# Ordering the modulation matmuls of a two-layer diffusion backbone on TensorE

## The chip, the cores and the metric

One core of one Trainium2 chip runs the whole program in one launch. The metric is device microseconds from the first to the last instruction of that core. The time before is the median of three runs, 2419.5 us (2418.51 to 2420.97).

## What is computed

Two streams of 128 tokens (context and latent) go through two trunk layers with the same weights. Each layer normalises its input, shifts and scales it by a vector that comes from a conditioning vector, makes one wide projection, runs three mixers on its columns, projects and merges their outputs, and adds the result to its input under a gate:

```python
mod = c_silu @ w_mod[l] + b_mod[l]                      # [1, 3*2048] of each stream
shift, scale, gate = jnp.split(mod, 3, axis=-1)
h = rms_norm(x, p['norm_w'][l]) * (1 + scale[:, None, :]) + shift[:, None, :]
(... 12 groups of columns ...) = split_columns(h @ p['w_in'][l])
# HGRN2 recurrence, grouped-query attention, S5 state-space scan
merged = (g_hg * (o_hg @ p['w_br_hg'][l]) + g_at * (o_at @ p['w_br_at'][l]) + g_s5 * (o_s5 @ p['w_br_s5'][l]))
x = x + gate[:, None, :] * (merged @ p['w_out'][l])
```

`mod` is what the change is about: one row of each stream times a matrix of 2048 x 6144, for each of the two layers. All values are float32.

## The kernel before

**The large products** are in `gemm` (lines 160 to 181). A piece of weights, `raw`, is 128 x 1024 (two chunks of 128 rows by 512 columns, 512 KB). SyncE issues its load; three `raw` buffers exist. Each chunk is split into a high part `wh` (a cast on ScalarE, line 138) and a low part `wl` (a subtraction on VectorE, line 139), four buffers each. TensorE then makes six matmuls of 128 x 512 for a chunk (lines 178, 179, 180 for each of the two streams), into a PSUM tile `g`. There are 672 pieces and 8064 of these matmuls.

**The modulation** is in `mod_part` (lines 244 to 295). `w_mod` is cut in six parts a layer, of 1024 columns each, and sixteen chunks of 128 rows. Since only two rows are on the left, a chunk is done as four matmuls, each with 32 columns of the array and 256 columns of the weights, at `tile_position=(0, 32 * i)`: four of them stand side by side in the array and write four partition blocks of one PSUM tile `mod`. A run of chunk pairs is summed in PSUM, and VectorE adds the sum to `bm` (line 276). The first part of layer 0 is done before everything else, parts 1 to 3 run beside the first columns of the projection, one pair of chunks (8 matmuls) at a time. The other eight parts (the gate of layer 0 and all of layer 1) run as *side work* of the later `gemm` calls: a generator is advanced by a rate, and each step loads four chunks (`MB = 2` pairs) and makes their 16 matmuls: 32 bursts of 16. Their weights `wm` go into buffers of 128 x 1024 that the tags `k4` (three buffers) and `q4` (two) hold, which other tiles use as well: five chunks at most stand ready at a time. The loads are issued by SyncE, in one queue with those of `raw`.

**The order** on each engine is made by a scheduler that simulates the program: of the instructions that are ready in its simulated time it takes the one with the lowest priority number. `self.prio(base)` numbers what stands in it from `base` upwards in order of writing. Loads and splits have `P_TOP` (1,000,000), the matmuls of `gemm` and those of the side work `P_PE` (6,000,000), the S5 scan on VectorE `P_SCAN` (500,000), and `P_MIX` is 0. An engine works its instructions in that order and waits where one is not ready.

**The S5 scan** (line 820 on) is 64 dependent steps of four VectorE instructions (lines 825, 827, 830, 831), made eight times in all; `bu` matmuls (line 813) feed it, and `yp` matmuls (lines 837 and 844) on TensorE need its end.

Of the kernel before, what the change touches and what calls it, by code (L numbers as in the profile page):

```python
# [52 lines left out]
P_MIX = 0  # L53
# [8 lines left out]
class Builder:  # L62
# [65 lines left out]

# [1 line left out]
    def transpose4(self, src, n=4, ps=None):  # L130
# [29 lines left out]
    def gemm(self, pieces, hi, lo, nk):  # L160
        """hi(k), lo(k): [128, 256] stationary parts of both streams; pieces: DRAM APs [128, 1024]."""
        nc = self.nc
        ps = [self.pg.tile([128, 512], F32, tag="g", name=self.nm("g")) for _ in range(2)]
        for kk, src in enumerate(pieces):
            self.side_work()
            with self.prio(P_TOP):
                raw = self.wp.tile([128, 2, 512], F32, tag="raw", name=self.nm("raw"), bufs=RAW)
                nc.sync.dma_start(raw, src.rearrange("p (a b) -> p a b", a=2))
            for j in range(2):
                with self.prio(P_TOP):  # L170
                    wh = self.wp.tile([128, 512], F32R, tag="wh", name=self.nm("wh"))
                    wl = self.wp.tile([128, 512], F32R, tag="wl", name=self.nm("wl"))
                    self.split_from(raw[:, j], wh, wl)
                k = 2 * kk + j
                with self.prio(P_PE):
                    for s in range(2):
                        sl = slice(s * 128, s * 128 + 128)
                        nc.tensor.matmul(ps[s], lo(k)[:, sl], wh, start=(k == 0), stop=False)  # L178
                        nc.tensor.matmul(ps[s], hi(k)[:, sl], wh, start=False, stop=False)  # L179
                        nc.tensor.matmul(ps[s], hi(k)[:, sl], wl, start=False, stop=(k == nk - 1))  # L180
        return ps

    def rstd(self, ssq, n, width):
        """1/sqrt(ssq/width + eps), with one Newton step after the table's square root."""
        nc = self.nc
        v = self.ts("v", (128, n))
        y = self.ts("y", (128, n))
        r = self.ts("r", (128, n))
        w = self.ts("w", (128, n))
        nc.vector.tensor_scalar(v, ssq, 1.0 / width, EPS, ALU.mult, ALU.add)  # L190
        nc.scalar.activation(y, v, AF.Sqrt)
        nc.vector.reciprocal(r, y)
        nc.vector.tensor_mul(w, r, r)
        nc.vector.tensor_mul(w, w, v)
        nc.vector.tensor_scalar(w, w, -0.5, 1.5, ALU.mult, ALU.add)
        nc.vector.tensor_mul(r, r, w)
        return r

# [1 line left out]
    def condition(self):  # L200
# [41 lines left out]

# [1 line left out]
    def mod_part(self, l, part, prio, tags, plan):  # L244
        """A sixth of c @ w_mod for both streams, two k chunks at a time; four column blocks side by side.

        Parts 0 to 3 are shift and scale of a quarter of the channels, 4 and 5 the halves of the gate. plan: runs
        of chunk pairs that are summed in PSUM, (bank, pairs, pairs between two yields)."""
        nc, io = self.nc, self.io
# [5 lines left out]
        for bank, run, burst in plan:  # L255
            ps = None
            for k0 in range(kb, kb + run, burst):
                ws = []
                for k in range(k0, k0 + burst):
                    with self.prio(P_TOP):  # L260
                        tag, n = next(tags)
                        for i in range(0, 2, n):
                            w = self.t(tag if isinstance(tag, str) else tag[i], "wm", (128, n * 1024))
                            nc.sync.dma_start(w, io["w_mod"][l, part, k][:, i * 1024:(i + n) * 1024])
                            ws += [w[:, j * 1024:(j + 1) * 1024] for j in range(n)]
                with self.prio(prio):
                    if ps is None:
                        pool = dict(g=self.pg, m=self.pm, b=self.pb)[bank]
                        ps = pool.tile([128, 512], F32, tag=bank, name=self.nm("mod"))
                    for k in range(2 * k0, 2 * (k0 + burst)):  # L270
                        for i in range(4):
                            nc.tensor.matmul(ps[32 * i:32 * i + 32, 0:256], self.cT[:, 2 * k:2 * k + 32],  # L272
                                             ws[k - 2 * k0][:, i * 256:i * 256 + 256], start=(k == 2 * kb),
                                             stop=(k == 2 * (kb + run) - 1), tile_position=(0, 32 * i))
                    if k0 + burst == kb + run:
                        nc.vector.tensor_add(bm, bm, ps[:, 0:256])
                if k0 + burst < 8:
                    yield True
            kb += run
# [16 lines left out]

# [1 line left out]
    def square(self, ssq, x, s, n):  # L298
# [9 lines left out]
    def normed(self, x, rs, q):  # L308
        """Channels 512 q .. 512 q + 511 of both streams."""
        nc = self.nc  # L310
# [20 lines left out]
    def in_group(self, l, name, idx, k0=0, k1=16):  # L331
        """Channel chunks k0 .. k1 - 1 of one group of columns."""
        pieces = [self.io["w_in"][l, GIDX[name, idx], kk] for kk in range(k0 // 2, k1 // 2)]
# [7 lines left out]
    def begin(self, l, name, idx, q):  # L341
        """A quarter of the channels' share of a group, put where the whole will stand."""
        ps = self.in_group(l, name, idx, 4 * q, 4 * q + 4)
# [40 lines left out]

# [1 line left out]
    def hgrn_unit(self, l, s, hf, q, f, v, og):  # L386
        """Four heads of one stream. q, f[2] (sigmoids), v: [128 tokens, 512]; og: output slice [128, 512].

        Pairs (s, t) are covered by a binary tree over time: at level m the queries of one half of every
        2m-block meet the keys of the other half; QF/KB carry the decay from the block's inner edge."""  # L390
        nc, io = self.nc, self.io
# [97 lines left out]

# [1 line left out]
    def head_norm(self, x, nh, w):  # L491
# [22 lines left out]
    def attention(self, l, s, q, kv, og):  # L514
        """q: [128, 8, 128], kv: [128, 512] (2 key heads, 2 value heads); og: [128, 1024]."""
        nc, io = self.nc, self.io
# [57 lines left out]

# [1 line left out]
    def vexp(self, x, n, wk):  # L576
        """exp on the vector engine to float32 accuracy."""
        nc = self.nc
# [60 lines left out]
    def s5_params(self, l):  # L639
        """Discretised per-state coefficients of both directions.  # L640

        The scan runs over pairs of tokens: state' = a^2 state + (a B u_first + B u_second)."""
        nc, io = self.nc, self.io
# [61 lines left out]
    def s5_input(self, l, qd, Bl, C, Sb):  # L705
        """Input matrices of one quarter, block-diagonal over two groups, the odd token's part stacked on the
        even one's; built in the scan's buffer before the scan needs it."""
        nc, io = self.nc, self.io
# [34 lines left out]
    def s5_output(self, l, qd, C, CC, cb):  # L743
        """C a of both directions, and C B + diag(d), which joins a token to its own output."""
        nc = self.nc
# [18 lines left out]
    def s5_half(self, l, hh, us, ys):  # L764
        """Channels of chunks 4*hh .. 4*hh+3 of both streams; us[s]: [128 tokens, 512]."""
        nc = self.nc
# [88 lines left out]

# [1 line left out]
    def layer(self, l, x, rs):  # L857
# [247 lines left out]
def _tiles(w, ncol):  # L1105
    """[K, N] -> [N/ncol, K/256, 128, 2*ncol]: 128-row chunks in pairs, side by side."""
    k, n = w.shape
    return w.reshape(k // 256, 2, 128, n // ncol, ncol).transpose(3, 0, 2, 1, 4).reshape(
        n // ncol, k // 256, 128, 2 * ncol)


def _mod_parts(w):
    """Columns shift | scale | gate -> quarters of shift and scale together, halves of the gate."""
    h = D // 4
# [91 lines left out]
```

## Time and profile before

| | before |
|---|---|
| median of three runs | 2419.5 us |
| span of the profiled execution | 2418.4 us |
| TensorE busy | 2355.8 us (97%) |
| VectorE busy | 1812.5 us (75%) |
| ScalarE busy | 1185.1 us (49%) |
| HBM read | 474.36 MB, 199 GB/s over the span |

The profile is of one execution, and its span is 1.1 us below the median. Busy time is the union of an engine's instructions. A timeline row gives the start, the busy time of the row, and how many instructions it merges. On TensorE one float32 matmul of the modulation is recorded twice (two passes), so `x2` is one matmul of it and `x32` a burst of 16. The matmuls of `gemm` are recorded once each.

### The profile page before, as it was taken

The numbers are of one execution on the slowest core, as the hardware profiler recorded it, in microseconds if no ns is written. First come the engines' busy times: TensorE is split into PE (matmuls) and PEld (weight loads), VectorE is DVE, ScalarE is ACT, GpSimd is POOL, SyncE is SP. The second block draws the span as 40 slices with busy tenths as digits, with TensorE's granted clock in tenths as the row PEclk, the third lists the DMA queues.
The fourth block names the chain that finished last, engine by engine and source line by source line (L and its number), as shares of the span: only waits on it lengthen the run. The fifth ranks groups of instructions, "written<-read, shape, count | busy, mean of one in ns | idle before, by whom it ended". The sixth has DMA issues, their size and how long they took to land.

```text
span 2418.4 us, 38199 instructions
## 1 busy us (share of the span) xinstructions
PE 2355.8 (97%) x13192; PEld 1817.0 (75%) x13192; DVE 1812.5 (75%) x4835; ACT 1185.1 (49%) x2061; POOL 132.9 (5%) x244
## 2 busy tenths in 40 slices
PE   5999999999999999999998999999999999999997
PEld 2667878888786676677776888888888776687776
DVE  5855998799878768665565798899869868856555
ACT  3436645555553433444446555555564453354444
POOL 2000001000100100000010001000010010000000
PEclk9999999999999999999999999999999999999999
DMA  8994553345557767777864554354546656656665
GB/s 311 344 326 133 161 181 115 124 155 192 170 164 261 238 212 252 243 270 252 298 214 143 158 175 153 126 166 149 184 157 191 198 166 211 219 174 219 224 199 177
DMA packets 131490, 483.85 MB, mean 200 GB/s; under 512 B 17200, under 2 KB 17808, under 8 KB 126944
## 3 DMA queue, kind: packets, MB, share of 16 engines
q1 hardware_dynamic: 120528, 454.09, 57.0%
q0 software_dynamic: 9472, 23.97, 3.4%
q10 hardware_dynamic: 1296, 3.36, 0.4%
q8 instruction: 103, 1.69, 0.3%
q14 instruction: 91, 0.75, 0.1%
HBM read 474.36 MB, written 6.98 MB: 199 GB/s over the span
## 4 chain that ended last, share of the span: by engine, by line
PE 92%; DMA 3%; DVE 3%; issue 1%; ACT 1%; SPq 0%; DVEq 0%; ACTq 0%
PE g L178 26%; PE g L180 25%; PE g L179 25%; PE mod L272 5%; PE bu L813 2%; PE lv L429 2%; DMA raw<-w_in 2%; PE tr L134 2%; PE yp L844 1%; DVE wl L139 1%; DMA wm<-w_mod 1%; PE yp L837 1%; PE bt L731 1%; PE ao L569 0%; PE sc L553 0%
## 5 line engine op out<-in xcount | busy, mean ns | idle before, releaser
L138 ACT CAST wh<-raw 128x512 fp32r<-128x512 f32 x1344 | 823.1, 621 | 1005.9 <-PE g L179 759.5
L139 DVE TENSOR_TENSOR wl<-raw,wh 128x512 fp32r<-128x512 f32 x1344 | 916.0, 688 | 418.2 <-ACT wh L138 365.6
L178 PE MATMUL g<-wh,hl 128*128 128x512 f32 x1984 | 798.2, 402 | 4.9 <-ACT wh L138 2.4
L179 PE MATMUL g<-wh,hh 128*128 128x512 f32 x1984 | 787.4, 397 | 0.0
L180 PE MATMUL g<-wl,hh 128*128 128x512 f32 x1984 | 716.6, 404 | 0.0
L178 PEld LDWEIGHTS g<-wh,hl 128*128 128x128 f32 x1984 | 375.1, 189 | 117.7 <-ACT wh L138 17.8
L180 PEld LDWEIGHTS g<-wl,hh 128*128 128x128 f32 x1984 | 366.0, 189 | 97.4 <-DVE Sb L831 6.6
L179 PEld LDWEIGHTS g<-wh,hh 128*128 128x128 f32 x1984 | 375.3, 189 | 81.8 <-issue 0.4
L272 PE MATMUL mod<-wm,cs 128*32 128x256 f32 x1536 | 155.6, 406 | 22.8 <-DMA wm<-w_mod 16.2
L178 PE MATMUL g<-wh,ol 128*128 128x512 f32 x384 | 154.5, 402 | 0.0
L825 DVE TENSOR_TENSOR p<-s5sc,Sb 128x64 f32<-128x64 f32 x512 | 140.1, 274 | 16.1 <-ACT Sb L817 7.1
L179 PE MATMUL g<-wh,oh 128*128 128x512 f32 x384 | 150.1, 391 | 0.0
L831 DVE TENSOR_TENSOR Sb<-Sb,p 128x64 f32<-128x64 f32 x512 | 140.8, 275 | 8.7
L827 DVE TENSOR_TENSOR p<-s5sc,Sb 128x64 f32<-128x64 f32 x512 | 138.2, 270 | 0.0
L180 PE MATMUL g<-wl,oh 128*128 128x512 f32 x384 | 133.9, 394 | 0.0
L272 PEld LDWEIGHTS mod<-wm,cs 128*32 128x32 f32 x1536 | 50.0, 113 | 106.8 <-issue 54.9
L830 DVE TENSOR_TENSOR p<-p,p 128x64 f32<-128x64 f32 x512 | 112.8, 220 | 6.4
L178 PE MATMUL g<-wh,mt 128*128 128x512 f32 x256 | 101.6, 397 | 0.0
L179 PE MATMUL g<-wh,mt 128*128 128x512 f32 x256 | 101.1, 395 | 0.0
L178 PEld LDWEIGHTS g<-wh,ol 128*128 128x128 f32 x384 | 72.0, 188 | 26.1 <-ACT wh L138 7.7
L180 PE MATMUL g<-wl,mt 128*128 128x512 f32 x256 | 85.4, 400 | 1.2 <-DVE wl L139 1.2
L180 PEld LDWEIGHTS g<-wl,oh 128*128 128x128 f32 x384 | 71.2, 188 | 18.7 <-DVE Sb L831 1.6
(315 smaller groups left out, 2112.6 us busy)
## 6 DMA issues: line engine op xcount, KB each, us to landing
raw<-w_in SPq DMA_DIRECT2D x496, 512.0 KB, 3.8
wm<-w_mod SPq DMA_DIRECT2D x130, 512.0 KB, 5.1
raw<-w_br SPq DMA_DIRECT2D x96, 512.0 KB, 4.2
raw<-w_out SPq DMA_DIRECT2D x64, 512.0 KB, 4.4
wm<-w_mod SPq DMA_DIRECT2D x31, 1024.0 KB, 7.4
raw<-w_glu SPq DMA_DIRECT2D x16, 512.0 KB, 4.3
gb<-gate_d POOLq DMA_DIRECT2D x16, 256.0 KB, 6.4
x<-x ACTq DMA_DIRECT2D x2, 1024.0 KB, 14.4
```

The source lines that it names most:

```text
L134: nc.tensor.transpose(ps[:, k], src[:, k * 128:(k + 1) * 128], self.ident)
L138: self.nc.scalar.copy(hi, src)
L139: self.nc.vector.tensor_sub(lo, src, hi.bitcast(F32))
L178: nc.tensor.matmul(ps[s], lo(k)[:, sl], wh, start=(k == 0), stop=False)
L179: nc.tensor.matmul(ps[s], hi(k)[:, sl], wh, start=False, stop=False)
L180: nc.tensor.matmul(ps[s], hi(k)[:, sl], wl, start=False, stop=(k == nk - 1))
L272: nc.tensor.matmul(ps[32 * i:32 * i + 32, 0:256], self.cT[:, 2 * k:2 * k + 32], ws[k - 2 * k0][:, i * 256:i * 256 + 256], start=(k == 2 * kb),
L429: nc.tensor.matmul(ps[:, h], mix[:, h], view(Z, HT + h * 128, [[2 * m, nb], [2 * HT + m, 2], [1, m]]), start=True, stop=True)
L825: tt(p0.rearrange("p d (j s) -> p d j s", s=2), view(sc, qd * 32, [[16, 2], [1, 16], [0, 2]]), view(Sb, i, [[ds, 2], [2 * W, 16], [W, 2]]) ...
L827: tt(p1, view(sc, 128 + qd * 64, [[32, 2], [16, 2], [1, 16]]), view(Sb, i + RI, [[ds, 2], [-RI, 2], [W, 16]]), ALU.mult)
L830: tt(p0, p0, p1, ALU.add)
L831: tt(cur, cur, p0, ALU.add)
```

## The change

The matmuls of one step (four chunks of four matmuls for the side work, two chunks for the parts at the start) are written in the opposite order of chunks, so that the chunk whose load is written last comes first. The very first of them keeps the priority of its part; all the others get `P_MIX`, the lowest number there is. The accumulation flags follow the new order. Loads, tiles, buffers and the number of instructions stay as they are.

```diff
-                    for k in range(2 * k0, 2 * (k0 + burst)):
+                    for j, k in enumerate(reversed(range(2 * k0, 2 * (k0 + burst)))):
                         for i in range(4):
-                            nc.tensor.matmul(ps[32 * i:32 * i + 32, 0:256], self.cT[:, 2 * k:2 * k + 32],
-                                             ws[k - 2 * k0][:, i * 256:i * 256 + 256], start=(k == 2 * kb),
-                                             stop=(k == 2 * (kb + run) - 1), tile_position=(0, 32 * i))
+                            with self.prio(P_MIX if j + i else prio):
+                                nc.tensor.matmul(ps[32 * i:32 * i + 32, 0:256], self.cT[:, 2 * k:2 * k + 32],
+                                                 ws[k - 2 * k0][:, i * 256:i * 256 + 256], start=(k0 == kb and j == 0),
+                                                 stop=(k0 + burst == kb + run and j == 2 * burst - 1),
+                                                 tile_position=(0, 32 * i))
```

Lines after this place stand two lower in the changed file (its modulation matmul is L273). On TensorE, this is one piece of a burst in layer 0 before, where `mod` is the modulation, `g` the large products, and the numbers tell buffers apart:

```order
L272 MATMUL mod_2136_9277<-wm_2132_9269,cs_77 32x256 x2
L178 MATMUL g_2071_9015<-wh_2109_9177,hl_321_1765 128x512
L179 MATMUL g_2071_9015<-wh_2109_9177,hh_320_1764 128x512
L178 MATMUL g_2072_9016<-wh_2109_9177,hl_321_1765 128x512
L179 MATMUL g_2072_9016<-wh_2109_9177,hh_320_1764 128x512
L272 MATMUL mod_2136_9277<-wm_2132_9269,cs_77 32x256
L180 MATMUL g_2071_9015<-wl_2110_9178,hh_320_1764 128x512
L180 MATMUL g_2072_9016<-wl_2110_9178,hh_320_1764 128x512
```

The same burst on TensorE in the changed kernel:

```order
L180 MATMUL g_2072_9016<-wl_2087_9074,hh_38_553 128x512
L273 MATMUL mod_2136_9277<-wm_2135_9275,cs_77 32x256 x4
L273 MATMUL mod_2136_9277<-wm_2134_9273,cs_77 32x256 x4
L273 MATMUL mod_2136_9277<-wm_2133_9271,cs_77 32x256 x4
L273 MATMUL mod_2136_9277<-wm_2132_9269,cs_77 32x256 x4
L178 MATMUL g_2071_9015<-wh_2089_9085,hl_39_554 128x512
```

Before, the 16 matmuls of this burst stand in seven places between matmuls of `gemm`; now they stand in one, and earlier in the program. Over the whole program the modulation stands in 168 places before and in 64 now. The first 25 places (parts 0 to 3 of layer 0) are the same in both, in runs of 64 and 8. Behind them there are 143 places before (112 of 1 to 4 matmuls, 12 of 5 to 8, 11 of 9 to 12, 8 of 13 to 16) and 39 now (25 of 16, and seven bursts cut in 4 and 12).

SyncE's queue at the loads of that burst, before (`wm_2132` to `wm_2135` are its four chunks; `wm_2093` to `wm_2096` those of the burst ahead of it):

```order
L264 DMA wm_2095_9109<-w_mod 128x1024
L264 DMA wm_2096_9111<-w_mod 128x1024
L168 DMA raw_2088_9083<-w_in 128x1024
L264 DMA wm_2133_9271<-w_mod 128x1024
L168 DMA raw_2098_9131<-w_in 128x1024
L168 DMA raw_2103_9153<-w_in 128x1024
L264 DMA wm_2132_9269<-w_mod 128x1024
L168 DMA raw_2108_9175<-w_in 128x1024
L264 DMA wm_2135_9275<-w_mod 128x1024
L168 DMA raw_2113_9197<-w_in 128x1024
L264 DMA wm_2134_9273<-w_mod 128x1024
```

And SyncE's queue now:

```order
L168 DMA raw_2056_8941<-w_br 128x1024
L264 DMA wm_2133_9271<-w_mod 128x1024
L168 DMA raw_2066_8989<-w_br 128x1024
L264 DMA wm_2093_9105<-w_mod 128x1024
L264 DMA wm_2095_9109<-w_mod 128x1024
L168 DMA raw_2073_9017<-w_in 128x1024
L264 DMA wm_2096_9111<-w_mod 128x1024
L168 DMA raw_2078_9039<-w_in 128x1024
L168 DMA raw_2083_9061<-w_in 128x1024
L168 DMA raw_2088_9083<-w_in 128x1024
L264 DMA wm_2132_9269<-w_mod 128x1024
L264 DMA wm_2134_9273<-w_mod 128x1024
```

One chunk of a burst is loaded ahead, and the other three are now issued in a row, behind the burst that frees their buffers. The loads are the same in number and size.

## Rows read from the trace of the kernel before

**Rows 1.** The page's busy times: us (share of the span) and instructions.
```profile
span 2418.4 us, 38199 instructions
PE 2355.8 (97%) x13192; PEld 1817.0 (75%) x13192; DVE 1812.5 (75%) x4835; ACT 1185.1 (49%) x2061; POOL 132.9 (5%) x244
```

**Rows 2.** TensorE's own waits, 60 to 2400 us: total us, times, longest.
```profile
PE tr L134 <- DVE xn L319: 10.3, 3, 6.4
PE g L178 <- ACT wh L138: 2.4, 5, 1.2
```

**Rows 3.** Waits of all engines, whole span, same columns.
```profile
ACT wh L138 <- PE g L179: 759.5, 834, 3.7
```

**Rows 4.** TensorE's timeline around single matmuls of the modulation: start, busy us, instructions.
```profile
885.46 0.39 PE L180 MATMUL g<-wl,hh 128*128 128x512 f32 x1
885.78 0.62 PE L272 MATMUL mod<-wm,cs 128*32 128x256 f32 x2
886.33 0.50 PE L178 MATMUL g<-wh,hl 128*128 128x512 f32 x1
886.67 0.39 PE L179 MATMUL g<-wh,hh 128*128 128x512 f32 x1
886.90 0.40 PE L178 MATMUL g<-wh,hl 128*128 128x512 f32 x1
```

**Rows 5.** TensorE's timeline around eight matmuls in a row.
```profile
65.36 0.39 PE L180 MATMUL g<-wl,hh 128*128 128x512 f32 x1
65.68 1.07 PE L272 MATMUL mod<-wm,cs 128*32 128x256 f32 x16
...
67.02 0.39 PE L179 MATMUL g<-wh,hh 128*128 128x512 f32 x1
```

**Rows 6.** TensorE's timeline around a burst, 1149 to 1155 us.
```profile
1149.20 0.39 PE L180 MATMUL g<-wl,hh 128*128 128x512 f32 x1
1149.43 0.38 PE L134 MATMUL tr<-ident,bm 128*128 128x128 f32 x2
1149.56 0.48 PE L178 MATMUL g<-wh,hl 128*128 128x512 f32 x1
...
1152.25 0.40 PE L180 MATMUL g<-wl,hh 128*128 128x512 f32 x1
1152.58 1.93 PE L272 MATMUL mod<-wm,cs 128*32 128x256 f32 x30
...
1154.78 0.40 PE L179 MATMUL g<-wh,oh 128*128 128x512 f32 x1
```

**Rows 7.** TensorE busy by the modulation's line alone, in two stretches.
```profile
700.00:1250.00 550.00, 79.75 (x768) 26.15 (x768) 1.00 0.74 247
1900.00:2350.00 450.00, 34.71 (x256) 9.21 (x256) 1.00 0.62 202
```

**Rows 8.** SyncE's timeline: issues of loads before and behind the burst of rows 6.
```profile
1143.27 1.91 SPq L264 DMA_DIRECT2D wm<-w_mod  x4
...
1153.27 1.29 SPq L264 DMA_DIRECT2D wm<-w_mod  x3
```

**Rows 9.** The tile wm, 700 to 1250 us: issue to landing of its loads.
```profile
DMA to landing us min/median/max: 3.2/5.4/11.5
```

**Rows 10.** Stretches: length, busy PE, PEld, DVE, ACT, POOL, granted clock, DMA share, GB/s.
```profile
60.00:120.00 60.00, 60.00 (x384) 41.82 (x383) 51.37 (x260) 29.54 (x55) 1.56 (x4) 1.00 0.93 344
720.00:735.00 15.00, 15.00 (x73) 11.77 (x72) 14.24 (x39) 8.16 (x14) 0.00 (x0) 1.00 0.66 208
871.00:994.00 123.00, 123.00 (x605) 81.93 (x604) 103.56 (x336) 46.48 (x76) 3.54 (x7) 1.00 0.75 251
1800.00:1933.00 133.00, 133.00 (x589) 106.67 (x591) 121.51 (x361) 64.83 (x107) 1.45 (x4) 1.00 0.62 192
1995.00:2128.00 133.00, 133.00 (x581) 89.64 (x583) 109.93 (x331) 52.20 (x85) 4.05 (x8) 1.00 0.65 212
```

**Rows 11.** The page's group of the splits: busy us, mean ns of one, idle before.
```profile
L139 DVE TENSOR_TENSOR wl<-raw,wh 128x512 fp32r<-128x512 f32 x1344 | 916.0, 688 | 418.2 <-ACT wh L138 365.6
```

## The prediction

> **What bounds the kernel now.** I read the busy times first: TensorE is busy 2355.8 of 2418.4 us, VectorE 75%, ScalarE 49% [rows 1]. A busy share alone doesn't say who waits for whom, so I then read TensorE's own waits. From 60 us to the end the longest total is 10.3 us in three places, and the casts to `wh` make it wait 2.4 us in all [rows 2]. The other way round, ScalarE waits 759.5 us for TensorE to free its `wh` buffers [rows 3]. So TensorE is the bound nearly everywhere behind the start-up, and a microsecond that it need not spend comes off the end, until another engine or a load is late. None of TensorE's waits behind 60 us is for `wm`.
>
> **What a visit to the modulation costs.** The timelines show the price of leaving the large products for the modulation and coming back. Two neighbouring matmuls of `gemm` start 0.23 us apart [rows 4]. Around a single matmul of the modulation the starts run 885.46, (885.78), 886.33, 886.67: 1.21 us for two steps that would take 0.46, so the visit costs 0.75 us [rows 4]. Eight in a row cost 67.02 - 65.36 - 0.46 = 1.20 us [rows 5]. Fifteen in a row, four rounds of four places, cost 1154.78 - 1152.25 - 0.46 = 2.07 us [rows 6]. These three lie on one line: 0.32 us for the visit, and 0.43 us for each round of up to four matmuls side by side (0.75, 1.18, 2.04). One matmul alone costs a whole round, since the other three quarters of the array stand idle. The 0.32 belongs to the change between the narrow tiles and the full array: transposes that use the full array stand between two matmuls of `gemm` with 1149.20, 1149.43, 1149.56 and no such gap [rows 6]. It isn't a hidden wait for data either: the list of TensorE's waits has none for `wm` or `cs` there [rows 2], and ScalarE's casts run ahead [rows 3].
>
> **The change, term by term.** No instruction is added or removed. Nothing moves in the first 25 places of the modulation.
> - Visits: 143 become 39 behind the start, by the order on TensorE. 104 x 0.32 = 33.3 us less.
> - Rounds: before, 112 visits of one round, 12 of two, 11 of three, 8 of four, which is 112 + 24 + 33 + 32 = 201. After, 25 of four and seven of 1 + 3, which is 128. 73 x 0.43 = 31.4 us less.
> - Together 64.7 us. The modulation's own busy time checks it: in the two stretches that hold the bursts it is 79.75 + 34.71 = 114.5 us [rows 7], and 32 bursts of 1.93 us (the last row of fifteen stands for one [rows 6]) would be 61.8, so 52.7 us of it go, and what the visits cost outside their busy time (0.75 - 0.62 = 0.13 each [rows 4]) adds 104 x 0.13 = 13.5 us: 66.2 us.
>
> All of that lies on the path, as TensorE doesn't wait in these stretches. Against the profiled execution this is 2418.4 - 64.7 = 2353.7 us of span, and 1.1 us more for the median of the runs: 2354.8 us before anything is given back.
>
> **What it adds: a wait for the latest load.** A burst now begins with one chunk's first matmul and goes on without a break, so all of its four chunks must have landed, and they free their buffers within 2 us of each other. With five buffers only one chunk of the next burst can be there by then. The other three wait in SyncE's queue for the burst, with the loads of `raw` behind them; on TensorE all matmuls of `gemm` are queued behind the burst's first one, and the casts behind those through the four `wh` and `wl` buffers. So the question is whether three loads land between two bursts. Before, a burst's start at 1152.58 is followed by three issues from 1153.27 to 1154.56 [rows 6, 8], so the last issue is done 2.0 us after the burst's start, and a load lands 5.4 us after its issue at the median, 11.5 us at most [rows 9]: 7.4 us, at worst 13.5. By the order there are 36 to 52 matmuls of `gemm` between neighbouring bursts at 21 places, at the tightest 36, which is 36 x 0.23 + 2.07 = 10.4 us, and 44 in the mean, 12.2 us; elsewhere there are 60 and more. At the median landing nothing waits. At the worst landing everywhere, 1.3 us x 21 = 27 us would be given back. Below nothing there is no room: a load can't make TensorE faster than its own work. A precedent lies near the median: the four loads issued from 1143.27 to 1145.18 [rows 8] serve a burst whose last fifteen matmuls start at 1152.58 with no idle time ahead of them [rows 6]. The rate is asked for too: at the densest place, eight bursts long, the queue carries 25 pieces of `raw` and 29 of `wm`, 28.3 MB, in some 92 us of TensorE work (308 x 0.23 + 8 x 2.07 + 4), which is 310 GB/s. From 60 to 120 us the chip moved 344 GB/s with TensorE busy 60.00 of 60.00 us [rows 10]. I take 2 us, near the precedent.
>
> **What may be late next: the S5 scan.** Its 64 steps share VectorE with the splits, and `yp` on TensorE needs the last step. Two of the eight scans lie beside many bursts. From 871 to 994 us VectorE is busy 103.56 of 123 us, from 1995 to 2128 us 109.93 of 133 [rows 10], and TensorE is busy throughout. From the last `bu` of the scan to its `yp`, TensorE's visits there cost 30.8 us (33 of them) and 25.5 us (34), after the change 14.9 and 4.4; with 25 and 40 matmuls of `gemm` more on the way (5.8 and 9.2 us) it arrives 10.1 and 11.9 us sooner. VectorE then has 112.9 and 121.1 us for 106.5 and 114.5 us of work, counting 0.69 us for the split of each chunk more (six matmuls) [rows 11]: 94% and 95%. It has been as full as 14.24 of 15 us, 95%, with TensorE busy 15.00 of 15, and 121.51 of 133, 91%, over a whole scan [rows 10]. If it gets to 95%, nothing is late; at 91% the two scans end 4.1 and 4.7 us late. So 0 to 9 us are given back, and I take 4, between the two.
>
> The sum: 2354.8 + 2 + 4 = 2361 us.
>
> **Rivals.**
> - VectorE sets the pace in the two scans. If the four dependent instructions of a step, and not VectorE's occupancy, set its length, the scans take as long as now and the shortening of those two stretches is lost: 10.1 + 11.9 = 22 us instead of the 4, so 2354.8 + 2 + 22 = 2379 us. For it: in both stretches VectorE is busy only 83 to 84% [rows 10]. Against it: the same 64 steps ran at 91% elsewhere, and splits stand between the steps and fill their gaps.
> - Slower: the loads come too late at each burst. The place is the first matmul of a burst. The mean spacing is 12.2 us, and 2.0 of it pass before the last issue is done, so a landing time of 10.2 us is free; the sign turns where 21 waits eat 64.7 us, 3.1 us each, at landings of 13.3 us. With 16 us each burst waits 5.8, in all 122 us: 2354.8 + 122 = 2477 us. For it: three loads and then up to three of `raw` go out at once, and SyncE holds `raw` back while it waits. Against it: 5.4 us at the median and 11.5 at most [rows 9], and 310 GB/s is below what the chip has already moved [rows 10].
> - The change does only half of what it says: the 0.32 us were for something that a whole burst meets as well, and only the 73 rounds are saved: 2419.5 - 31.4 + 6 = 2394 us; against it speak the bursts of before, which lie on the same line.
>
> The Trainium skill, page "DMA: Bandwidth & Descriptors", section "Rules for kernel authors", says to issue a load early and to wait for it late, so that its fixed time is covered. The change does the reverse on both sides, since it frees the buffers together and begins with the chunk loaded last. That is the slower rival; no run here shows its price yet, and by that rule alone the sum would lose up to a landing time a burst, where the rows show that the spacing of the bursts covers it.
>
> **How the numbers follow.** My forecast, 2361 us, has a chance of 0.76, with a range of its own from 2350 (nothing given back, and 5 us of error in the prices) to 2391 (27 + 9 us given back). VectorE as the pace: 0.10. Half of the saving: 0.05. Slower: 0.05. The remaining 0.04 are for a mixture that ends near 2419. A measurement of this kernel can tell about 0.2%, 4.8 us, from no change. Faster by more than that: 0.76 + 0.10 + 0.05 = 0.91; within it 0.04; slower 0.05. The range 2350 to 2391 holds the forecast and the scan's rival.
>
> **What would show it.** In the changed profile the modulation's busy time from about 700 to 2350 us should fall from 114.5 to about 62 us, and its rows should read x32, x24 and x8 alone. TensorE's waits should show a few microseconds for `wm` and for the S5 tiles. If the slower rival is right, TensorE waits for `wm` at some twenty bursts, 3 us or more each, and the loads land after more than 13 us. If the scan's rival is right, `yp` or the splits wait for VectorE from 850 to 980 and from 1930 to 2080 us. I am wrong altogether if the modulation's time falls as said and the span doesn't: then TensorE waits for something that the rows of before don't show.

## The result, and the profile after

The changed kernel runs in 2357.1 us (median of four runs, 2356.7 to 2357.6), the kernel before in 2419.0 us on the same chip. The ratio is 0.9743, with a 95% interval of 0.973 to 0.9757. The forecast was 2361 us, with a range of 2350 to 2391. So 62 us went, and the first question is whether they went where the sum had put them.

The changed kernel's page, busy times (us, share of the span, instructions; PE is TensorE's matmuls, PEld its loads of the stationary part, DVE VectorE, ACT ScalarE, POOL GpSimd), and its group of the modulation's matmuls (busy us, mean ns of one, idle before):

```profile
span 2355.8 us, 38207 instructions
PE 2290.3 (97%) x13192; PEld 1818.4 (77%) x13192; DVE 1805.0 (77%) x4835; ACT 1180.3 (50%) x2061; POOL 133.7 (6%) x244
L273 PE MATMUL mod<-wm,cs 128*32 128x256 f32 x1536 | 103.5, 401 | 24.9 <-DMA wm<-w_mod 18.5
```

The same group on the page of before, which stood at L272:

```profile
L272 PE MATMUL mod<-wm,cs 128*32 128x256 f32 x1536 | 155.6, 406 | 22.8 <-DMA wm<-w_mod 16.2
```

TensorE executes the same 13192 matmuls as in [rows 1] and is busy for 65.5 us less (2355.8 to 2290.3). The span fell by 62.6 us. The difference of 2.9 us is time in which TensorE now stands idle. Of the 65.5 us, 155.6 - 103.5 = 52.1 are the modulation's own. The other 13.4 us fall to the matmuls beside it, which the sum had put at 104 x 0.13 = 13.5.

The modulation's line by itself, in the two stretches that hold the bursts (length, then busy PE and PEld with instructions, granted clock, DMA share, GB/s):

```profile
600.00:1250.00 650.00, 47.66 (x768) 22.26 (x768) 0.99 0.72 244
1850.00:2350.00 500.00, 15.68 (x256) 7.39 (x256) 1.00 0.63 208
```

These answer [rows 7]: the same 1024 records took 114.5 us and now take 63.3. Behind the start the timeline has 25 visits of x32, seven of x24 and seven of x8, as the prediction said.

A burst on TensorE after the change (start, busy us; two records are one matmul):

```profile
759.26 0.39 PE L179 MATMUL g<-wh,oh 128*128 128x512 f32 x1
759.48 0.61 PE L180 MATMUL g<-wl,oh 128*128 128x512 f32 x2
760.03 1.93 PE L273 MATMUL mod<-wm,cs 128*32 128x256 f32 x32
761.89 0.50 PE L178 MATMUL g<-wh,hl 128*128 128x512 f32 x1
762.23 0.39 PE L179 MATMUL g<-wh,hh 128*128 128x512 f32 x1
```

From 759.26 to 762.23 there are four steps between matmuls of `gemm` (the row at 759.48 holds two), 0.23 us each, and the visit: 2.97 - 0.92 = 2.05 us. That is the price of four rounds in [rows 6], unchanged: the change makes no visit cheaper, it makes fewer of them.

What TensorE waits for from 60 to 2400 us (total us, times, longest), and how long the loads of `wm` take from issue to landing from 600 to 1250 us:

```profile
PE tr L134 <- DVE xn L321: 10.3, 3, 6.4
PE g L178 <- ACT wh L138: 3.1, 6, 1.3
PE mod L273 <- DMA wm<-w_mod: 2.7, 4, 1.8
PE g L180 <- DVE wl L139: 1.2, 2, 0.8
DMA to landing us min/median/max: 3.6/7.2/11.7
```

Against [rows 2], one new kind of line of a size that counts is there: the first matmul of a burst waits for its load, four times, 2.7 us in all (0.3 us of it ahead of 400 us, at a burst of eight). The line for `wl` is not new, though [rows 2] leave it out: before, it was 1.2 us in two places as well. The loads land later than in [rows 9], at the median 7.2 us in place of 5.4; three or four of them now go out in a row. The longest takes 11.7 us, near the 11.5 of before.

Waits of all engines: ScalarE still waits for TensorE to free `wh`, though less than in [rows 3].

```profile
ACT wh L138 <- PE g L179: 625.8, 754, 3.8
```

So TensorE is still the bound, with 625.8 us of slack on the side of the casts.

### The profile page after: what moved, and what is told of

The parts are those of the page before. It is cut to its first block, busy times and chain, and to the rows that moved or that the text cites. A ratio compares the mean times of both kernels' runs of the same rounds, so it can differ in the third digit from the quotient of the medians.

```text
span 2355.8 us, 38207 instructions
## 1 busy us (share of the span) xinstructions
PE 2290.3 (97%) x13192; PEld 1818.4 (77%) x13192; DVE 1805.0 (77%) x4835; ACT 1180.3 (50%) x2061; POOL 133.7 (6%) x244
## 4 chain that ended last, share of the span: by engine, by line
PE 90%; DMA 5%; DVE 4%; issue 1%; ACT 1%; SPq 0%; DVEq 0%; ACTq 0%
PE g L178 25%; PE g L180 25%; PE g L179 25%; PE mod L273 3%; PE bu L815 2%; DMA wm<-w_mod 2%; PE lv L431 2%; PE tr L134 2%; DMA raw<-w_in 1%; PE yp L846 1%; DVE wl L139 1%; DMA raw<-w_br 1%; PE yp L839 1%; PE bt L733 1%; PE ao L571 0%
## 5 line engine op out<-in xcount | busy, mean ns | idle before, releaser
L138 ACT CAST wh<-raw 128x512 fp32r<-128x512 f32 x1344 | 819.1, 621 | 948.7 <-PE g L179 625.8
L273 PE MATMUL mod<-wm,cs 128*32 128x256 f32 x1536 | 103.5, 401 | 24.9 <-DMA wm<-w_mod 18.5
L273 PEld LDWEIGHTS mod<-wm,cs 128*32 128x32 f32 x1536 | 44.2, 113 | 76.0 <-DMA wm<-w_mod 23.7
```

What stands on the lines that cost most here:

```text
L138: self.nc.scalar.copy(hi, src)
```

## The experiments

Eleven runs were made, two of them of the changed kernel again, in three groups, each on one chip with the kernel before beside it (2419.3, 2419.8 and 2420.1 us there). Executions of one kernel spread by several microseconds on these chips, so a difference of a few is read from the traces and not from the medians.

**The changed kernel again**, the yardstick of the first group.

> The changed kernel itself, as the yardstick on this chip. Both theories: 2357 us (2355 to 2359), 0.974 to 0.975 of the kernel before.

Measured: 2362.5 us (2356.5 to 2365.1, four runs), ratio 0.9762 (0.9748 to 0.9777). TensorE is busy 2290.1 us in its profiled execution, which took 2356.5 us. So TensorE's time comes out again to 0.2 us in this execution, the fastest of the four, and the end times lie within some 9 us of each other. Of the slower ones there is no profile.

**Priority alone**: the chunks keep the order of before, but all matmuls behind a burst's first have the top priority.

```diff
-                    for j, k in enumerate(reversed(range(2 * k0, 2 * (k0 + burst)))):
+                    for j, k in enumerate(range(2 * k0, 2 * (k0 + burst))):
```

> Keeps the top priority of all but the first matmul and takes the reversal of the chunks back: the first chunk written comes first. By the order TensorE then has 50 places of the modulation behind the start instead of 39, with 128 rounds as before. The price line (0.32 us a visit, 0.43 us a round) gives 11 x 0.32 = 3.5 us more than the changed kernel: 2360.6 us. If the waits for the load of the last chunk were what matters, not to wait for it would win back the 2.7 us that TensorE waits for wm in the changed kernel, and the time would be 2354 to 2357 us.

Measured: 2360.1 us (2357.8 to 2363.2), ratio 0.9757 (0.9744 to 0.977). Its group of the modulation on the page, in the columns of above:

```profile
L273 PE MATMUL mod<-wm,cs 128*32 128x256 f32 x1536 | 106.1, 402 | 24.3 <-DMA wm<-w_mod 17.7
```

TensorE is busy 2296.5 us, 6.4 more than in the run of the changed kernel beside it, where eleven more visits had been priced at 3.5. In the runs' times the two can't be told apart.

**Reversal alone**: the last loaded chunk first, with the priorities of before.

```diff
-                            with self.prio(P_MIX if j + i else prio):
+                            with self.prio(prio):
```

> Keeps the reversal of the chunks and takes the priorities back: all matmuls of a burst have the priority of their part. By the order 125 places of the modulation behind the start (143 before the change, 39 with it) and 191 rounds (201 and 128). The price line: (125 - 39) x 0.32 + (191 - 128) x 0.43 = 54.6 us more than the changed kernel, 2411.7 us. If the reversal were what frees TensorE, by waiting once for the latest load, this would stay near 2357 us.

Measured: 2412.5 us (2409.6 to 2413.8, seven runs), ratio 0.9968 (0.9957 to 0.998).

```profile
L273 PE MATMUL mod<-wm,cs 128*32 128x256 f32 x1536 | 148.1, 407 | 23.6 <-DMA wm<-w_mod 17.1
```

So the price line holds between the ends as well, at 125 visits and 191 rounds. TensorE is busy 55.7 us more than in the changed kernel again on the first group's chip (2345.8 against 2290.1), where the price line had 54.6. The reversal by itself is worth 7 us of the 62, probably since fewer matmuls can start before the last chunk is there. With the priorities on, it is worth a few microseconds at most. The top priority of the matmuls behind the first does the work.

**Bursts of eight**: two chunks next to each other instead of four.

```diff
-MB = 2
+MB = 1
```

> Steps of one pair of chunks instead of two (MB = 1), so bursts of 8 instead of 16; the sums into bm on VectorE double from 32 to 64. By the order 62 places instead of 39, 128 rounds in both. The price line: 23 x 0.32 = 7.4 us more, 2364.5 us. The theory that only the rounds cost (the saving of half the size) expects no more than the sums' VectorE time can delay: 2357 to 2359 us. The theory that the loads set the pace expects it to be faster than the changed kernel, since half a burst needs only two loads: 2352 to 2356 us.

Measured: 2365.2 us (2362.5 to 2366.6), ratio 0.9776 (0.9762 to 0.9789).

```profile
PE 2297.4 (97%) x13192; PEld 1813.7 (77%) x13192; DVE 1816.3 (77%) x4867; ACT 1184.2 (50%) x2061; POOL 135.7 (6%) x244
L273 PE MATMUL mod<-wm,cs 128*32 128x256 f32 x1536 | 109.1, 405 | 22.3 <-DMA wm<-w_mod 15.8
```

62 visits with the same 128 rounds cost 7.3 us more of TensorE than 39, where 23 x 0.32 = 7.4 had been the price. TensorE never waits for `wm` behind the start here. Bursts of eight already have all the full rounds (31.4 us of the sum) and 81 of the 104 avoided visits (25.9 us); the second doubling buys 7 us and has a few waits for loads with it.

**Larger bursts at the start**: parts 1 to 3 of layer 0, which the change leaves in 24 runs of eight, in bursts of 16.

```diff
-                    yield from self.mod_part(0, p, P_CHAIN, itertools.cycle(STAGS), [("b", 8, 1)])
+                    yield from self.mod_part(0, p, P_CHAIN, itertools.cycle(STAGS), [("b", 8, 2)])
-            self.start_side(parts(), SRATE)
+            self.start_side(parts(), SRATE / 2)
```

> Parts 1 to 3 of layer 0, which run beside the first projections in bursts of 8, run in bursts of 16 (their rate is halved with it). By the order 13 places of the modulation at the start instead of 25, the rounds as before. The price line: 12 x 0.32 = 3.8 us less than the changed kernel, 2353.3 us, if the loads keep up there. The loads' theory: two loads of 1 MB must land for each burst in the stretch where the queue already moves 340 GB/s, so the 12 bursts wait up to 2 us each and the time is 2357 to 2380 us.

Measured: 2360.8 us (2358.8 to 2362.1, five runs), ratio 0.9759 (0.9746 to 0.9773): no faster, as far as the runs can tell, than the changed kernel beside it, whose lowest run is 2356.5. The expectation missed. Up to matmul 432 of `gemm`, where the edited bursts lie, the profiled execution takes 182.0 us and that of the changed kernel 183.5: 1.5 us less, not 3.8, and at matmul 500 only 0.3 us of it are left. TensorE's waits and its clock show most of the rest. Its waits from 60 to 400 us, one row of its timeline, and a stretch in the columns of [rows 10]:

```profile
PE tr L134 <- DVE modT L294: 2.8, 1, 2.8
PE mod L273 <- DMA wm<-w_mod: 1.1, 1, 1.1
89.81 1.93 PE L273 MATMUL mod<-wm,cs 128*32 128x256 f32 x32 [1.15 <-DMA wm<-w_mod]
179.90:186.70 6.80, 5.60 (x15) 4.42 (x16) 2.90 (x8) 2.74 (x6) 0.00 (x0) 0.50 0.45 142
```

In the changed kernel a wait of 1.9 us for `xn` stands in place of the 2.8 for `modT`, and `wm` is waited for 0.6 us. So 0.9 + 0.5 = 1.4 us go to a part's result that comes later and to a load. Around the longer wait TensorE's granted clock is 0.50, the lower of its two levels (1.2 GHz), for 6.8 us; in the changed kernel it is there from 182.3 to 185.7 us, for 3.4. At that level neighbours of `gemm` start 0.43 us apart (184.33, 184.76, 185.19) in place of 0.23, which makes some 1.2 us for the six neighbours more that run at it, an estimate from these starts. From 432 on the two programs' orders are alike. Behind matmul 500 the profiled execution loses another 3.5 us; two profiled executions of the changed kernel differ by up to 4 us on parts of that way, so this may be the spread; no run shows that it is.

**One column block after the other**: the sixteen matmuls of a burst ordered so that all four chunks of one column block come before the next block. Same instructions, same visits, no four neighbours on different quarters of the array.

```diff
-                    for j, k in enumerate(reversed(range(2 * k0, 2 * (k0 + burst)))):
-                        for i in range(4):
-                            with self.prio(P_MIX if j + i else prio):
+                    ks = list(enumerate(reversed(range(2 * k0, 2 * (k0 + burst)))))
+                    order = [(j, k, i) for i in range(4) for j, k in ks] if burst == MB else [
+                        (j, k, i) for j, k in ks for i in range(4)]
+                    for n, (j, k, i) in enumerate(order):
+                        with self.prio(P_MIX if n else prio):
```

> The bursts of 16 stay together, but their order inside is turned: the four chunks of the first block of 32 columns, then those of the second, and so on, so that neighbours no longer stand side by side in the array. By the order 38 places. If a round is up to four matmuls side by side and costs 0.43 us, each burst now takes 13 to 16 rounds instead of 4: 32 x 12 x 0.43 = 165 us more at most, 2490 to 2522 us, and slower than the kernel before. If the 0.43 is paid for each four instructions whatever their places, the time stays at 2357 us.

Measured: 2440.0 us (two runs, 2439.97 and 2440.08), ratio 1.0083 (1.0062 to 1.0103), slower than the kernel before. TensorE around one of its bursts, and the page's group:

```profile
734.57 0.40 PE L179 MATMUL g<-wh,hh 128*128 128x512 f32 x1
734.89 4.59 PE L275 MATMUL mod<-wm,cs 128*32 128x256 f32 x32
739.42 0.73 PE L180 MATMUL g<-wl,hh 128*128 128x512 f32 x2
739.99 0.40 PE L178 MATMUL g<-wh,hl 128*128 128x512 f32 x1
L275 PE MATMUL mod<-wm,cs 128*32 128x256 f32 x1536 | 188.5, 401 | 22.7 <-DMA wm<-w_mod 16.1
```

The visit costs 739.99 - 734.57 - 3 x 0.23 = 4.73 us in place of 2.05, without a wait for a load. So keeping the matmuls together isn't enough: neighbours must lie on different quarters of the array. (Each quarter writes its own place in PSUM, so the runs don't tell the quarter from the place.) The size missed. I had expected sixteen rounds of 0.43 us. The records of this burst show why it is less: each matmul is two passes, passes of one chain start 0.216 us apart, and after the first four passes a second chain runs beside the first (starts at 0, 0.24, 0.46, 0.67, 0.89 and a second one at 0.89 us). Two passes then run at once for 12 steps, and the last four run alone: 20 steps of 0.216 us are 4.3. That the second chain is the next column block is inferred, since the records don't name the block.

**A burst on the full array**: the bursts' stationary part is 128 columns wide and not 32, so that no narrow tile is entered or left. It sums all four column blocks into one place, which is not the modulation; the number of matmuls is the same.

```diff
+                                if bank == "m":
+                                    nc.tensor.matmul(ps[:, 0:256], self.cT[:, 2 * k:2 * k + 128],
+                                                     ws[k - 2 * k0][:, i * 256:i * 256 + 256], start=(j + i == 0),
+                                                     stop=(j == 2 * burst - 1 and i == 3))
+                                else:
...
```

> The matmuls of the bursts use the whole array: 128 columns of the left side (the columns behind the two streams' hold other chunks or zeros), all four blocks of a chunk summed into one PSUM region, so what comes out as modulation is not the reference's. The burst stays together, in 33 places by the order, but no two matmuls stand side by side, and there is no change between narrow tiles and the full array. Theory of the tile change: a visit of n matmuls costs n x 0.43 us and nothing on top, so the step from a matmul of gemm to the first of the burst is 0.23 us and not 0.33, and the visit's own 0.32 us is gone; in all 512 x 0.43 - 67.5 = 153 us more than the changed kernel, 2510 us. If the 0.32 us belonged to the change of operands or of the PSUM tile, it would stay: 33 x 0.32 = 10.6 us more, 2520 us, and 0.33 us at the step into the burst.

Measured: 2505.7 us (two runs, 2504.5 and 2507.0), ratio 1.0354 (1.0333 to 1.0375). The time lies below both theories' numbers, nearer to the 2510 of the tile change; TensorE's busy time is 153.3 us above the changed kernel's, where that theory had 153. The page's busy times, and TensorE around a burst:

```profile
PE 2443.6 (98%) x13192; PEld 1987.2 (79%) x13192; DVE 1823.6 (73%) x4835; ACT 1185.7 (47%) x2060; POOL 133.5 (5%) x244
890.85 0.39 PE L179 MATMUL g<-wh,hh 128*128 128x512 f32 x1
891.08 0.40 PE L180 MATMUL g<-wl,hh 128*128 128x512 f32 x1
891.32 7.07 PE L274 MATMUL mod<-wm,cs 128*128 128x256 f32 x32
898.04 0.58 PE L178 MATMUL g<-wh,ol 128*128 128x512 f32 x1
898.46 0.39 PE L179 MATMUL g<-wh,oh 128*128 128x512 f32 x1
```

The first matmul of the burst follows 0.24 us behind the one of `gemm`, like any neighbour, where 0.32 or 0.33 us stand ahead of a narrow one [rows 4 to 6]. The whole visit costs 898.46 - 891.08 - 0.46 = 6.92 us, and 16 x 0.43 is 6.9. Nothing is left for entering and leaving. So the 0.32 us of a visit is the price of the change between narrow tiles and the full array, and this run shows it. The Trainium skill, page "TensorEngine Tiling (Array Packing)", section "Key Properties", says that TensorE is drained when the tiling mode changes; the two kinds of visit agree with that, and give it a price of 0.32 us there and back.

The loads of the stationary part (PEld) show where it goes. The first row is the burst on the full array, the other two are the changed kernel's burst of above:

```profile
891.15 0.37 PEld L274 LDWEIGHTS mod<-wm,cs 128*128 128x128 f32 x2
760.03 1.45 PEld L273 LDWEIGHTS mod<-wm,cs 128*32 128x32 f32 x32 [0.35 <-PE g L180]
761.89 0.19 PEld L178 LDWEIGHTS g<-wh,hl 128*128 128x128 f32 x1 [0.41 <-issue]
```

On the full array the first load starts at 891.15, 0.17 us ahead of its matmul (891.32) and beside the last one of `gemm`. At the narrow burst it starts together with its matmul (760.03), and so does the first load behind the burst (761.89). How much of the 0.32 us is a load that isn't covered, and how much something else at the change, these runs don't separate.

**One buffer fewer, and one more.** The third group asks how near the loads are to setting the pace. Four buffers for `wm` in place of five:

```diff
-MTAGS = ((("k4", "q4"), 1), (("k4", "q4"), 1), (("k4", "k4"), 1))
+MTAGS = ((("k4", "q4"), 1),)
-                         mo=1, st=10, k2=6, k4=3, gt=4, sm=18, s5i=4, p=4, sb=1, sc=1, s5t=1)
+                         mo=1, st=10, k2=6, k4=2, gt=4, sm=18, s5i=4, p=4, sb=1, sc=1, s5t=1)
```

> The changed kernel again, as the yardstick of the next three runs on the same chip: 2357 us, TensorE busy 2290 us, waits for wm of 1.5 to 2.7 us in all. The three differ from it in the number of buffers for wm alone (five here: three of k4, two of q4).

> One buffer for wm fewer, four in all: none of a burst's chunks can be there before the burst ahead of it has run, so four loads have to be issued and land between two bursts and not three. By the order, the bursts begin 36 to 44 matmuls of gemm apart at some twenty places, most of them cut in 4 and 12: 47 visits behind the start and not 39, which is 8 x 0.32 = 2.6 us. Theory of the near edge (the loads' late arrival is the price at which the change would stop to pay, and five buffers are just enough): a fourth load costs 0.4 us more to issue and, at 340 GB/s, 1.5 us more to move, so a landing of 7.2 us at the median becomes about 9, behind 2.4 us of issues: 11.4 us where 36 to 44 matmuls take 8.4 to 10.2 us. TensorE then waits 1 to 3 us for wm at each of some twenty bursts, and the time is 2357 + 2.6 + 20 to 60 = 2380 to 2420 us. Theory of ample cover (the spacing covers four loads as well): waits for wm of 5 us at most in all, 2360 to 2365 us.

Measured: the changed kernel 2358.4 us (2357.1 to 2361.3), ratio 0.9747 (0.9732 to 0.9761); four buffers 2370.3 us (2368.6 to 2371.8), ratio 0.9794 (0.9778 to 0.9811). Neither theory has the time, but the waits decide between them. TensorE's waits for `wm` from 400 us on, where all the bursts of 16 lie, with four buffers:

```profile
PE mod L273 <- DMA wm<-w_mod: 1.9, 3, 0.8
```

and in the changed kernel beside it:

```profile
PE mod L273 <- DMA wm<-w_mod: 1.3, 2, 0.9
```

The fourth load costs the bursts of 16 0.6 us of waiting in all, not 20 to 60. The spacing of the bursts covers four loads, and the near edge falls. The 12 us come from elsewhere. TensorE's waits for `wm` from 60 us on, the longest of them, and a stretch in the columns of [rows 10], all with four buffers:

```profile
PE mod L273 <- DMA wm<-w_mod: 6.0, 5, 2.7
181.60 1.94 PE L273 MATMUL mod<-wm,cs 128*32 128x256 f32 x16 [2.68 <-DMA wm<-w_mod]
798.50:801.90 3.40, 3.40 (x10) 2.62 (x8) 3.30 (x12) 0.01 (x1) 0.00 (x0) 0.50 0.67 239
```

Up to matmul 432 of `gemm` this kernel takes 188.5 us and the changed one 184.7: its order puts the last two bursts of eight of the start one right behind the other, and they wait 4.0 us for their loads, though their buffers are none of those taken away. From number 2200 to number 3790 it takes 461.6 us and the changed one 453.4. There it has ten more visits, 3.2 us by the price, as its order cuts 17 bursts in 4 and 12 where seven were cut. Behind a wait of 1.9 us for `wl` the granted clock is 0.50 from 798.5 to 801.9 us, where eight steps of `gemm` take 3.39 us and not 8 x 0.23 = 1.84, so some 1.5 us are the clock's, by this estimate. The rest, some 3 us, can't be assigned by these runs.

Six buffers, paid for with two of `k2`, and then with one of `k2` and one of `gt`:

```diff
-MTAGS = ((("k4", "q4"), 1), (("k4", "q4"), 1), (("k4", "k4"), 1))
+MTAGS = ((('k4', 'q4'), 1), (('k4', 'k4'), 1))
-                         mo=1, st=10, k2=6, k4=3, gt=4, sm=18, s5i=4, p=4, sb=1, sc=1, s5t=1)
+                         mo=1, st=10, k2=4, k4=4, gt=4, sm=18, s5i=4, p=4, sb=1, sc=1, s5t=1)
```

> One buffer for wm more, six in all, paid for with two small buffers of k2 (four and not six). Two chunks of a burst can be there ahead, and no burst is cut any more: 32 visits behind the start and not 39, 128 rounds as before. By the price of a visit 7 x 0.32 = 2.2 us of TensorE's busy time go (2288 us), and by the near edge theory the waits for wm go too (1.5 to 2.7 us): 2352.5 us. If the fewer k2 buffers make VectorE or ScalarE late, or if the waits for wm come back where the bursts now lie 30 to 40 matmuls apart, it is 2357 us or more, and TensorE's list of waits shows which.

> Six buffers for wm as well, paid for in another way: five buffers of k2 and three of gt in place of six and four. Same 32 visits and 128 rounds, 2352.5 us by the price of a visit and the near edge. If this run and the one with four of k2 agree, the sixth buffer is what they show; if only one of them is faster than the changed kernel, it is the buffers taken away that decide.

Measured: 2357.6 us (2351.7 to 2359.7), ratio 0.9738 (0.9722 to 0.9753), and 2359.9 us (2357.9 to 2360.8), ratio 0.975 (0.9736 to 0.9765). Neither can be told from the changed kernel's 2358.4. The first one's page and its waits for `wm` from 60 us on:

```profile
span 2354.4 us, 38214 instructions
PE 2289.7 (97%) x13192; PEld 1819.2 (77%) x13192; DVE 1806.2 (77%) x4835; ACT 1181.8 (50%) x2061; POOL 133.9 (6%) x244
PE mod L273 <- DMA wm<-w_mod: 0.6, 1, 0.6
```

The effect is there, and small. All 32 bursts run whole, none of them waits for `wm` (the 0.6 us lie ahead of 400 us), and TensorE's busy time is 1.4 us below the changed kernel's on this chip (2291.1), where 2.2 had been priced. Between matmuls 2200 and 3790 of `gemm` it takes 447.8 us and not 453.4. It is 1.7 us behind the changed kernel when it gets there, gains 2.1 us more up to matmul 6505 and loses 2.9 us behind it, so its profiled execution ends 3.0 us sooner in all. No version here is faster than the changed kernel by more than the measurement can tell.

## Why the prediction was right, step by step

- **What bounds the kernel.** Right: TensorE's busy time fell by 65.5 us and the span by 62.6, so what TensorE saved came off the end nearly in full.
- **The price of a visit and of a round.** Right, and tested at 50, 62 and 125 visits: expected 2360.6, 2364.5 and 2411.7 us, measured 2360.1, 2365.2 and 2412.5. That the first two come so near is partly luck, since they were worked out from 2357 us and the changed kernel beside them took 2362.5. The traces decide: TensorE's busy time follows the price to 0.1 us with bursts of eight (7.3 for 7.4), to 1.1 with the reversal alone (55.7 for 54.6), and to 2.9 with the priority alone (6.4 for 3.5). The step that assigned the 0.32 us to the tile change was argued from the transposes in [rows 6]; the visits on the full array show it.
- **The sum of 64.7 us, checked by 66.2.** TensorE's busy time gave 65.5, between the two. The modulation's own part of it was to be 52.7 and is 52.1 on the page; in the two stretches it was to fall to about 62 us and fell to 63.3. The 62 counted every burst at 1.93 us, also the seven that are cut in 4 and 12, whose two pieces take 0.64 and 1.50 us.
- **The loads, 2 us given back.** 2.7 us in the profiled execution, 1.5 and 1.3 in two others: the right size. The mean was within the spacing as the sum had it, though the landing time itself rose from 5.4 to 7.2 us, which the sum had not counted. The spacing has room for that: 2.0 + 7.2 = 9.2 us are still below the 10.4 us of the tightest place, and even four loads cost the bursts of 16 only 1.9 us of waiting.
- **The S5 scan, 4 us given back.** Mis-sized: nothing was given back. The two scans run from 860.5 to 972.1 and from 1944.5 to 2068.1 us (first to last step), 8.5 and 12.8 us shorter than before, where TensorE was to arrive 10.1 and 11.9 us sooner. The stretches, in the columns of [rows 10]:

```profile
860.50:972.10 111.60, 111.18 (x638) 82.90 (x637) 100.59 (x335) 44.84 (x76) 0.71 (x1) 1.00 0.84 294
1944.50:2068.10 123.60, 123.60 (x581) 98.51 (x580) 115.56 (x352) 57.95 (x96) 2.83 (x5) 1.00 0.65 214
```

VectorE is busy 90% and 93% of them and TensorE isn't held up: its only wait in the first is 0.3 us for a load, and in the second there is none. The step took 91% over a whole scan [rows 10] as a limit that VectorE might not pass. It was only the fullest that had been seen, and it was read too low: that stretch, 1800 to 1933 us, reaches some 6 us behind the end of its scan. Over the scan alone the kernel before has

```profile
1800.30:1927.40 127.10, 127.10 (x560) 103.24 (x559) 119.43 (x358) 62.89 (x104) 0.00 (x0) 1.00 0.61 190
```

which is 94%, near the 94 and 95% that the prediction worked out for the two scans. (Its second stretch, 1995 to 2128, begins 8 us inside its scan, which runs from 1987.2 to 2124.7; VectorE is 84% busy over that too.) Without this term the sum would have been 2357 us, which is the measured time. That it meets it to a few tenths is luck in part: the changed kernel's medians on three chips are 2357.1, 2358.4 and 2362.5 us.

- **The rival that the scan sets the pace (2379).** Wrong, by the same two rows: the scans got shorter as TensorE did. VectorE had slack that its busy share of 83% showed and the dependent steps did not take up.
- **The slower rival (2477).** Wrong, with room to spare. Its waits of 3 us at some twenty bursts are four waits of 2.7 us in all; landings stay at 11.7 us at most, below the 13.3 where the sign would turn, and a load more in each burst of 16 adds 0.6 us. The rule of the Trainium skill it rested on (page "DMA: Bandwidth & Descriptors", section "Rules for kernel authors": issue early, wait late) holds as a direction: before, TensorE had no wait for `wm` behind 60 us, and now it has. Its price here is 1.3 to 2.7 us against a saving of 65.
- **The rival of half the saving (2394).** Wrong: the 0.32 us of each avoided visit is saved, as the bursts of eight against those of sixteen show (7.3 us for 23 visits).

## What to carry to other kernels

On an engine that is the bound, count how often a stream of small matmuls on narrow tiles interrupts a stream on the full array, and how many neighbours fill each round; both prices can be read from three places in a trace and multiplied. Make the interruptions few and full by the order of the program, but look at what the burst's buffers and results are needed for: where the next step waits for the sum itself, as at the start here, a larger burst gave nearly all of its saving back. The highest busy share seen on another engine is no limit, and shouldn't be priced as one; and a share that is to speak for a stage must be read over that stage alone, from its first step to its last.

## What the runs showed of the hardware

- Narrow matmuls side by side do not need to be neighbours in groups of four to overlap at all: with one column block after the other two passes still ran at a time for 12 of 20 steps (that they belong to two blocks is inferred), and a burst of 16 took 4.73 us, between 2.05 (four at a time) and the 6.9 of one at a time.
- A matmul of 256 columns in f32 is 0.43 us on the full array as on a quarter of it (6.92 us for 16), so on narrow tiles the whole gain comes from the neighbours.
- The change between narrow tiles and the full array costs 0.32 us there and back, and there is no such price between a burst on the full array and the large products (6.92 us for 16 x 0.43). At the change the load of the stationary part starts together with its matmul (760.03 and 761.89 us) and not ahead of it (891.15 for 891.32).
- Around a wait of 2.8 us ahead of 181.1 us TensorE's granted clock was 0.50 for 6.8 us, and behind one of 1.9 us at 797.7 us for 3.4 us; neighbours of `gemm` then start 0.42 to 0.43 us apart in place of 0.23.
